# Zeroed sums and two borrowed weight places in the expert stage of a one-core trunk

## Chip, cores and metric

The kernel runs on one core of a Trainium2 chip. The metric is the device time of one launch in microseconds (us); lower is better. Before the change three timed runs gave 1368.88, 1369.80 and 1372.61 us, median 1369.8 us.

## What is computed

256 tokens of width 1024 pass a retention layer with a dense SwiGLU, and then an attention layer with a mixture of experts. The last part is what the change touches:

```python
logits = (xt @ w_router)                       # 256 tokens, 8 experts
top_val, top_idx = lax.top_k(logits, TOP_K)    # 2 of 8 for each token
gates = ...softmax of the two values...
for e in range(N_EXPERTS):                     # w_in[e]: 1024 x 7168, w_out[e]: 3584 x 1024, float32
    y = y + gates[:, e:e + 1] * swiglu(xt, w_in[e], w_out[e])
x = layer_norm(DEEPNORM_ALPHA * x + y)
```

The weights of the eight experts are 352 MB in float32, and every one of them is read once.

## The kernel before

**Experts, blocks and the flag.** For each expert the kernel gathers the rows (tokens) that chose it, at most 96 (CAP), as NB = 3 blocks of 32 rows. Blocks are the stationary operand of TensorE, weights are streamed past them. Block 2 (the third) is needed only where an expert has over 64 rows. That is known on the chip alone: VectorE writes a flag for each expert (`over`, `over_o`), TensorE loads it into a register (`third`), and `by_need` puts most of block 2's matmuls into a branch on it (L1195). The experts are taken in an order worked out on the chip (`which`), so their weights' addresses are registers.

**Units.** An expert's inner width of 3584 is cut into units of 2048 and 1536 columns (UNITS). A unit has a gate product `pg` and an up product `pu` (`gemm_e`, 8 steps of 128 rows of w_in each, tile `pe`, one PSUM bank a block), SiLU by ScalarE (L1266), a multiplication and a transpose by VectorE (L1288, L1290, tile `hT`), and the down product (`down`, 16 or 12 steps, tiles `po`, two banks for three blocks). The down product of a unit is issued after the up product of the next unit. Behind the second unit's down product `rows_of` copies the sums with ScalarE and VectorE (L1236 to L1243), and `scatter` adds them to `xa` one unit later. All matmuls of `gemm_e` and `down` are at L1176, in `mm_tiles`: 4 matmuls a step and block, which work on four column groups side by side. The profile counts each of them twice, since a float32 matmul is two instructions.

**`by_need`.** Steps are taken in groups (2 steps in the very first unit, else 4; 8 in the down product). In a group blocks 0 and 1 come first and then, in the branch, block 2. Step 0 is an exception: all three blocks run outside the branch, because its first matmul (start=True) is what sets block 2's sums to a value; its `done`, which gives the weight's place back, also comes ahead of the branch.

**Places and the stream of loads.** All weights pass through one `Stream`. A load is one DMA of 1 MB (or 0.75 MB, for the unit of 1536 columns), issued by SyncE (SP) at L217 in the order of use. `pump` issues a load as soon as a place is free; `Slots` counts the free places of a pool. Places come from `raws` (6), `raw_mid` (6), `raw_end` (3, free when the attention ends) and `base` (4, free when the attention's output product is done): 19 in the expert stage. A place is free again when the step that reads it is done. SP takes its list in order: a load that waits holds up all loads behind it. Loads use eight completion semaphores in turn, so a load also waits for the one eight before it.

**The attention's input.** `xT_h` and `xT_l` (1 MB each, pool `xtp`) hold the split, transposed input of the attention's products (L379 to L406). After the attention `xT_h`'s place is taken by `xa`, the residual of the last norm, written by ScalarE in `router_rest`, and `xT_l`'s place by `hT`.

**The end.** In the last expert TensorE adds `xa` into PSUM (L1304), runs the last down product, and scatters; VectorE and ScalarE then make the norm and store.

Of the kernel before, what the change touches and what calls it, by code (L numbers as in the profile page):

```python
# [23 lines left out]
P = 128  # L24
S = 256
D = 1024
# [71 lines left out]
class Slots:  # L98


    def __init__(self, pool, free, tag="raw"):
        self.pool, self.free, self.tag = pool, free, tag


class Stream:
# [78 lines left out]
def trunk_kernel(ctx, tc, x, ret_w_in, ret_w_out, sb_w_kv, sb_w_q, sb_w_out, ln_mix_g, ln_mix_b,  # L184
# [17 lines left out]
    def wtile(name="pw"):  # L202
        return psw.tile([P, 512], F32, tag="pw", name=nm(name))
# [665 lines left out]
    with att:  # L869
# [70 lines left out]
        for u in range(8):  # L940
            if u == 6:
                dst = [wtile("pv") for _ in range(2)]
                gemm_tok(dst, lambda t: keep_v(1, t, dst[t]))
            kq_half(u, 0)
            if u in (1, 2):
                att_a(u - 1)
            if u >= 2:
                att_c(u - 2)
            kq_half(u, 1)
            if u >= 2:  # L950
                att_e(u - 2)
                att_a(u)
        hl0 = st.take(4)
        acc0 = [wtile("sacc") for _ in range(2)]

# [21 lines left out]
        st.pump()  # L977


        xa = xtp.tile([P, 2, D], F32, tag="xT_h", name="xa")  # L980
        rt = mp.tile([P, P], F32, tag="gT0", name="rt")
        lg, rank, mask, ex = [rt[:, 64 + 16 * i:80 + 16 * i].rearrange("p (t e) -> p t e", t=2) for i in range(4)]
        mb = consts.tile([P, 2, NE], BF, name="mb")
# [141 lines left out]
        def router_rest():  # L1125

            nc.vector.tensor_scalar(mask, rank, 1.5, None, OP.is_lt)
            nc.vector.tensor_mul(ex, ex, mask)
            nc.vector.tensor_reduce(mx, ex, axis=AX.X, op=OP.add)
            nc.vector.reciprocal(mx, mx)  # L1130
            nc.vector.tensor_tensor(gates, ex, mx.rearrange("p (t o) -> p t o", o=1).to_broadcast((P, 2, NE)),
                                    OP.mult)
            nc.vector.tensor_reduce(nm_f, pc[:, :8], axis=AX.X, op=OP.max)
            nc.vector.tensor_copy(nmax, nm_f)
            turns()
            nc.vector.tensor_scalar(p2, p1, float(CAP), None, OP.subtract)
            for t in range(2):
                for n in range(2):
                    nc.vector.tensor_add(xs[t][:, half(n)], xs[t][:, half(n)], gb[1][n])
                nc.scalar.activation(xa[:, t, :], xs[t], AF.Copy, scale=ALPHA)  # L1140

        st.raws.append(base)
        st.pump()
# [3 lines left out]
        xg = gather_T(first)  # L1147
        nc.scalar.preload_act_table_set("silu_and_others")


    def slots(g, e, gates, last=False):

# [13 lines left out]
                nc.scalar.copy(gT[t], p[:, t * P:(t + 1) * P])  # L1166
        return gT, gs

    def mm_tiles(nb, o, lhs, cols, first, last, shared=False):

        for r in nb:
            for c, w in enumerate(cols):
                ov = o[r][c * 32:(c + 1) * 32]
                if len(w.shape) == 3:
                    ov = ov.rearrange("p (b j) -> p b j", j=w.shape[2])
                nc.tensor.matmul(ov, lhs[r], w, start=first and not (shared and r == 1), stop=last,  # L1176
                                 skip_group_check=True)

    def by_need(s, nk, group, third, mm):

        if third is None:
            for k in range(nk):
                mm(range(NB), k, s.take()[0])
                s.done()
            return
        for k0 in range(0, nk, group):
            ks = range(k0, min(k0 + group, nk))
            w = s.take(len(ks))  # L1190
            for k in ks:
                mm(range(NB - (k > 0)), k, w[k - k0])
            if k0 == 0:
                s.done()
            with tc.If(third > 0):  # L1195
                for k in ks:
                    if k > 0:
                        mm(range(NB - 1, NB), k, w[k - k0])
            for k in ks:
                if k > 0:  # L1200
                    s.done()

    def gemm_e(s, xg, n, third, group=4):


        o = [wtile("pe")[:, :n // 4] for _ in range(NB)]
        by_need(s, KD, group, third, lambda nb, k, w: mm_tiles(nb, o, [xg[:, r, k, :] for r in range(NB)], blocks(w, 64),
                                                        k == 0, k == KD - 1))
        return o

    def down(s, hT, nk, po, first, last, third):
        by_need(s, nk, 8, third, lambda nb, k, w: mm_tiles(nb, po, [hT[:, r, k, :] for r in range(NB)],
                                                        [w[:, c * 256:(c + 1) * 256] for c in range(4)],
                                                        first and k == 0, last and k == nk - 1, True))

    def alternate(o):

# [40 lines left out]
    def experts(s, pos, gates, g, xg, norm, hook=None, most=None, third0=None):  # L1258
        pend = done = po = None
        third = [third0] + [None] * (NE - 1)  # L1260
        for e in range(NE):
            for u, (c0, n) in enumerate(UNITS):
                hs = mp2.tile([P, NB, 512], F32, tag="hs", name=nm("hs"))[:, :, :n // 4]
                pg = gemm_e(s, xg, n, third[e], 2 if (e, u) == (0, 0) else 4)
                for r in range(NB):
                    nc.scalar.activation(pairs(hs[:, r, :]), alternate(pg[r]), AF.Silu)  # L1266
                if hook is not None:
                    hook()
                    hook = None
                if most is not None and (e, u) == (4, 0):  # L1270
                    most.append(nc.values_load(nmax[0:1, 0:1], min_val=0, max_val=S))
                if u == 1:
                    if done is not None:
                        scatter(*done)
                    sl = slots(g, e, gates, most is not None and e == NE - 1)
                    if e + 1 < NE:
                        if third0 is not None:
                            third[e + 1] = flag(over_o, e + 1)
                        g = one_hot(e + 1, pos)
                        nxt = gather(g)  # L1280
                pu = gemm_e(s, xg, n, third[e], 2 if (e, u) == (0, 0) else 4)
                if most is not None and (e, u) == (0, 0):
                    which[1:] = [nc.values_load(which_t[0:1, i:i + 1], engines=[SP], min_val=0, max_val=NE - 1,
                                                skip_runtime_bounds_check_because="a rank among NE")
                                 for i in range(1, NE)]
                hT = xtp.tile([P, NB, 16, 32], F32, tag="xT_l", name=nm("hT"))[:, :, :n // P]
                for r in range(NB):
                    nc.vector.tensor_mul(pairs(hs[:, r, :]), pairs(hs[:, r, :]), alternate(pu[r]))  # L1288
                for r in range(NB):
                    nc.vector.transpose(hT[:, r].rearrange("p k s -> p (k s)"), hs[:, r, :])  # L1290
                if pend is not None:
                    if pend[1] == 0:
                        po = new_po()
                    down(s, *pend[0], po, pend[1] == 0, pend[1] == 1, third[e - (u == 0)])
                    if pend[1] == 1:
                        done = (rows_of(po, sl[1]), sl[0])
                pend = ((hT, n // P), u)
            if e + 1 < NE:
                xg = nxt
        if most is not None:  # L1300
            sums = [[wtile("psc") for _ in range(2)] for _ in range(2)]
            for t in range(2):
                for n in range(2):
                    nc.tensor.matmul(sums[t][n], ident, xa[:, t, half(n)], start=True, stop=False)  # L1304
            tc.mark_branch_hint_location("more", 0, engines=[e for e in ENGINES if e != PE])
        down(s, *pend[0], po, False, True, third[NE - 1])
        if most is None:
            scatter(rows_of(po, sl[1]), sl[0], norm)
            for t in range(2):
                norm[t].fast_rstd(t == 1)  # L1310
            return None
        keep_warm(WARM[3], ident, ident)
        rows = rows_of(po, sl[1], True)
        for t in range(2):
            for n in range(2):
                nc.tensor.matmul(sums[t][n], sl[0][t][:CAP], rows[n][0], start=False, stop=True)
                nc.vector.bn_stats(norm[t].st[:, n, :], sums[t][n])
                nc.scalar.copy(xa[:, t, half(n)], sums[t][n])
            norm[t].fast_rstd(t == 1)
        return sums  # L1320

    norm = [Norm(t, [], xa[:, t, :]) for t in range(2)]
    for t in range(2):
        norm[t].st = small.tile([P, 2, 6], F32, tag="st", name=nm("st"))
    most = []
# [77 lines left out]
```

## Time and profile before

| What | Value |
|---|---|
| Median of the timed runs | 1369.8 us |
| Profiled execution, its own time | 1371.01 us |
| Its span (first to last instruction) | 1369.2 us |
| TensorE (PE) busy | 1325.5 us, 97% |
| VectorE (DVE), ScalarE (ACT) busy | 33%, 23% |
| DMA queue of SP | 442.01 MB, 82.8% of 16 engines |

The profile is one execution of the same program. PE busy means that a matmul was in the array or queued behind operands, so 97% is not a measure of how far the weights' loads leave TensorE waiting. The view by stretches gives, for each, busy time of every engine with the number of instructions, TensorE's granted clock (1.00 is 2.4 GHz, 0.50 is 1.2 GHz), the mean busy share of the 16 DMA engines and the bytes moved. A load's landing is the time of the last of its sixteen parts.

### The profile page before, as it was taken

The numbers are of one execution on the slowest core, as the hardware profiler recorded it, in microseconds if no ns is written. First come the engines' busy times: TensorE is split into PE (matmuls) and PEld (weight loads), VectorE is DVE, ScalarE is ACT, GpSimd is POOL, SyncE is SP. The second block draws the span as 40 slices with busy tenths as digits, with TensorE's granted clock in tenths as the row PEclk, the third lists the DMA queues.
The fourth block names the chain that finished last, engine by engine and source line by source line (L and its number), as shares of the span: only waits on it lengthen the run. The fifth ranks groups of instructions, "written<-read, shape, count | busy, mean of one in ns | idle before, by whom it ended". The sixth has DMA issues, their size and how long they took to land. (4 is left out here: it accounts for less than half of the span.)

```text
span 1369.2 us, 30767 instructions
## 1 busy us (share of the span) xinstructions
PE 1325.5 (97%) x13611; PEld 865.6 (63%) x13611; DVE 446.5 (33%) x652; ACT 314.8 (23%) x465; POOL 46.7 (3%) x73
## 2 busy tenths in 40 slices
PE   9999999999999999999989999999999999999986
PEld 7888889999989884354434454563644563554543
DVE  6746667555565554101201200201200200210213
ACT  6544435444437642000100100100100100100101
POOL 0212101000010000000000000000000000000000
PEclk9999999999999999999999999999999999999999
DMA  9865437555649357999999999999999999999993
GB/s 336 295 213 179 160 97 272 179 190 185 185 127 357 131 183 295 393 418 417 418 418 418 416 420 418 417 418 419 400 418 420 406 418 420 401 417 419 405 415 155
DMA packets 122918, 447.40 MB, mean 327 GB/s; under 512 B 9088, under 2 KB 56976, under 8 KB 92048
## 3 DMA queue, kind: packets, MB, share of 16 engines
q1 hardware_dynamic: 121808, 442.01, 82.8%
q0 software_dynamic: 960, 3.15, 0.7%
q8 instruction: 123, 2.02, 0.6%
q14 instruction: 27, 0.22, 0.0%
HBM read 444.08 MB, written 1.05 MB: 325 GB/s over the span
## 5 line engine op out<-in xcount | busy, mean ns | idle before, releaser
L1176 PE MATMUL pe<-raw,xg 128*32 128x384 f32 (+1 forms) x5248 | 506.3, 540 | 13.4 <-PEq L1195 7.4
L1176 PEld LDWEIGHTS pe<-raw,xg 128*32 128x32 f32 x5248 | 203.9, 110 | 305.4 <-issue 266.6
L1176 PE MATMUL po<-raw,hT 128*32 128x256 f32 x4544 | 254.4, 379 | 8.4 <-DMA raw<-in_moe_w_out_dram 5.4
L269 DVE TENSOR_TENSOR w<-raw,w 128x1024 fp32r<-128x1024 f32 x162 | 198.1, 1234 | 144.5 <-ACT w L268 142.2
L1176 PEld LDWEIGHTS po<-raw,hT 128*32 128x32 f32 x4544 | 170.0, 110 | 95.6 <-issue 10.7
L268 ACT CAST w<-raw 128x1024 fp32r<-128x1024 f32 x162 | 168.4, 1048 | 134.6 <-issue 32.1
L1288 DVE TENSOR_TENSOR hs<-hs,pe 128x512 f32<-128x512 f32 (+1 forms) x48 | 29.1, 620 | 362.9 <-PE pe L1176 361.2
L1266 ACT ACTIVATE hs<-pe 128x512 f32<-128x512 f32 (+1 forms) x48 | 25.3, 544 | 457.7 <-PE pe L1176 457.7
L404 PE MATMUL pf<-xT_h,w 128*128 128x256 f32 x448 | 126.9, 283 | 0.0
L406 PE MATMUL pf<-xT_l,w 128*128 128x256 f32 x448 | 126.2, 282 | 0.0
L405 PE MATMUL pf<-xT_h,w 128*128 128x256 f32 x448 | 126.1, 281 | 0.0
L1290 DVE STREAM_TRANSPOSE hT<-hs 128x512 f32<-128x512 f32 (+1 forms) x48 | 27.2, 617 | 237.6 <-PE po L1176 139.2
L404 PEld LDWEIGHTS pf<-xT_h,w 128*128 128x128 f32 x448 | 84.4, 188 | 0.3
L405 PEld LDWEIGHTS pf<-xT_h,w 128*128 128x128 f32 x448 | 84.4, 188 | 0.3
L406 PEld LDWEIGHTS pf<-xT_l,w 128*128 128x128 f32 x448 | 84.4, 188 | 0.0
L1236 ACT COPY y<-po 32x256 f32<-32x256 f32 x48 | 17.5, 364 | 283.3 <-PE po L1176 238.7
L379 PE MATMUL pv<-w,xT_l 128*128 128x512 f32 x96 | 38.4, 400 | 0.0
L381 PE MATMUL pv<-w,xT_h 128*128 128x512 f32 x96 | 38.0, 396 | 0.3 <-DVE w L269 0.3
L380 PE MATMUL pv<-w,xT_h 128*128 128x512 f32 x96 | 37.9, 395 | 0.0
L404 PE MATMUL pq<-xT_h,w 128*128 128x256 f32 x128 | 36.3, 283 | 0.0
L406 PE MATMUL pq<-xT_l,w 128*128 128x256 f32 x128 | 36.0, 281 | 0.0
L405 PE MATMUL pq<-xT_h,w 128*128 128x256 f32 x128 | 36.0, 281 | 0.0
(237 smaller groups left out, 1180.5 us busy)
## 6 DMA issues: line engine op xcount, KB each, us to landing
raw<-in_moe_w_in_dram SPq DMA_DIRECT2D x128, 1024.0 KB, 19.9
raw<-in_moe_w_out_dram SPq DMA_DIRECT2D x112, 1024.0 KB, 19.8
raw<-in_moe_w_in_dram SPq DMA_DIRECT2D x128, 768.0 KB, 15.8
raw<-in_ret_w_in_dram SPq DMA_DIRECT2D x22, 1024.0 KB, 9.3
raw<-in_ffn_w_in_dram SPq DMA_DIRECT2D x20, 1024.0 KB, 5.1
raw<-in_ffn_w_out_dram SPq DMA_DIRECT2D x11, 1024.0 KB, 5.0
raw<-in_ret_w_out_dram SPq DMA_DIRECT2D x8, 1024.0 KB, 5.0
raw<-in_sb_w_kv_dram SPq DMA_DIRECT2D x4, 1024.0 KB, 6.0
```

The lines of the kernel that those rows point to most:

```text
L268: nc.scalar.copy(hv, v)
L269: nc.vector.tensor_sub(lv, v, hv.bitcast(F32))
L379: nc.tensor.matmul(o, sl, mh, start=first, stop=False)
L380: nc.tensor.matmul(o, sh, mh, start=False, stop=False)
L381: nc.tensor.matmul(o, sh, ml, start=False, stop=last)
L404: nc.tensor.matmul(o, lo[:, k, :], xT_h[:, k, :], start=(k == 0), stop=False)
L405: nc.tensor.matmul(o, h[:, k, :], xT_h[:, k, :], start=False, stop=False)
L406: nc.tensor.matmul(o, h[:, k, :], xT_l[:, k, :], start=False, stop=(k == KD - 1))
L1176: nc.tensor.matmul(ov, lhs[r], w, start=first and not (shared and r == 1), stop=last, skip_group_check=True)
L1266: nc.scalar.activation(pairs(hs[:, r, :]), alternate(pg[r]), AF.Silu)
L1288: nc.vector.tensor_mul(pairs(hs[:, r, :]), pairs(hs[:, r, :]), alternate(pu[r]))
L1290: nc.vector.transpose(hT[:, r].rearrange("p k s -> p (k s)"), hs[:, r, :])
```

## The change

Three things are changed together.

1. *Zeroed sums.* Where there is a flag, VectorE sets block 2's sums to 0: 128x512 or 128x384 of a `pe` bank ahead of each `gemm_e`, and 128x256 of `po` ahead of the first unit's down product. Block 2's matmuls no longer start with start=True, and step 0's are in the branch with the others. All `done` of a group now come behind the branch.
2. *Two places more.* At the end of the attention two places of 1 MB, at `xT_l` and `xT_h`, are put among the `raws`. A `Once` place is given once: when its load has been used it does not come back.
3. *`xa` and `po` elsewhere in the order.* `xa` is made and written by ScalarE behind the up product of the first unit, not in `router_rest`; `new_po` comes ahead of the multiplications and transposes.

```diff
+class Once:
+    def __init__(self, pool, tag):
+        self.pool, self.tag, self._free = pool, tag, 1
...
+    @free.setter
+    def free(self, n):
+        self._free = min(self._free, n)
...
+        st.raws += [Once(xtp, tag) for tag in ("xT_l", "xT_h")]
+        st.pump()
         hl0 = st.take(4)
...
-                nc.scalar.activation(xa[:, t, :], xs[t], AF.Copy, scale=ALPHA)
...
+    def new_xa(norm):
+        nonlocal xa
+        xa = xtp.tile([P, 2, D], F32, tag="xT_h", name="xa")
+        for t in range(2):
+            norm[t].x = xa[:, t, :]
+            nc.scalar.activation(xa[:, t, :], xs[t], AF.Copy, scale=ALPHA)
...
             for k in ks:
-                mm(range(NB - (k > 0)), k, w[k - k0])
-            if k0 == 0:
-                s.done()
+                mm(range(NB - 1), k, w[k - k0])
             with tc.If(third > 0):
                 for k in ks:
-                    if k > 0:
-                        mm(range(NB - 1, NB), k, w[k - k0])
+                    mm(range(NB - 1, NB), k, w[k - k0])
             for k in ks:
-                if k > 0:
-                    s.done()
+                s.done()
...
         o = [wtile("pe")[:, :n // 4] for _ in range(NB)]
+        if third is not None:
+            nc.vector.memset(o[NB - 1], 0.0)
...
+                if pend is not None and pend[1] == 0:
+                    po = new_po()
+                    if third[e] is not None:
+                        nc.vector.memset(po[NB - 1], 0.0)
```

In the orders below a tile's number only tells copies apart, and line numbers of the changed kernel are its own (its L232 is L217 of before, L1200 is L1176, L1217 is L1195). The first place is SP's list at the end of the attention, with what each load waits for (DMAHW: an earlier load, DVE or PE: an engine). Before:

```order
L217 DMA raw_4372<-in_moe_w_in_dram 128x2048 [waits DMAHW5_49,DVE_49]
L217 DMA raw_4474<-in_moe_w_in_dram 128x2048 [waits DMAHW6_49,DVE_49]
L217 DMA raw_4568<-in_moe_w_in_dram 128x2048 [waits DMAHW7_49,DVE_49]
L217 DMA raw_4599<-in_moe_w_in_dram 128x2048 [waits DMAHW0_49,DVE_49]
L217 DMA raw_4617<-in_moe_w_in_dram 128x2048 [waits DMAHW1_49,PE_49]
L217 DMA raw_4619<-in_moe_w_in_dram 128x2048 [waits DMAHW2_49,PE_49]
```

And now:

```order
L232 DMA raw_4372<-in_moe_w_in_dram 128x2048 [waits DMAHW5_49,DVE_49]
L232 DMA raw_4474<-in_moe_w_in_dram 128x2048 [waits DMAHW6_49,DVE_49]
L232 DMA raw_4504<-in_moe_w_in_dram 128x2048 [waits DMAHW7_49,PE_49]
L232 DMA raw_4506<-in_moe_w_in_dram 128x2048 [waits DMAHW0_49]
L232 DMA raw_4572<-in_moe_w_in_dram 128x2048 [waits DMAHW1_49,DVE_49]
L232 DMA raw_4603<-in_moe_w_in_dram 128x2048 [waits DMAHW2_49,DVE_49]
```

Two loads (raw_4504, raw_4506) have come in behind the tenth load of the stage; they wait for TensorE's last reading of the attention's input. They are the eleventh and twelfth in the order of use; every later load stands two places further on in the list of places.

The second place is TensorE's list at the first gate product. Before:

```order
L1176 MATMUL pe_4857<-raw_3726,xg_4849 32x512 x4
L1176 MATMUL pe_4858<-raw_3726,xg_4849 32x512 x4
L1176 MATMUL pe_4859<-raw_3726,xg_4849 32x512 x4
L1176 MATMUL pe_4857<-raw_3808,xg_4849 32x512 x4
L1176 MATMUL pe_4858<-raw_3808,xg_4849 32x512 x4
L1195 COMPARE_AND_BRANCH
L1176 MATMUL pe_4859<-raw_3808,xg_4849 32x512 x4
```

And now:

```order
L1200 MATMUL pe_4860<-raw_3726,xg_4852 32x512 x4
L1200 MATMUL pe_4861<-raw_3726,xg_4852 32x512 x4
L1200 MATMUL pe_4860<-raw_3808,xg_4852 32x512 x4
L1200 MATMUL pe_4861<-raw_3808,xg_4852 32x512 x4
L1217 COMPARE_AND_BRANCH
L1200 MATMUL pe_4862<-raw_3726,xg_4852 32x512 x4
L1200 MATMUL pe_4862<-raw_3808,xg_4852 32x512 x4
```

Block 2's four matmuls of step 0 have moved behind the branch.

The third place is VectorE's list in the second unit of the sixth expert, between the transposes of the first unit's result and the gather of the next expert. Before:

```order
L1290 STREAM_TRANSPOSE hT_9698<-hs_9460 128x512 x3
L1236 COPY y_9863<-po_9248 32x256 x2
L1236 COPY y_9863<-po_9249 32x256
L1243 SCALAR_TENSOR_TENSOR y_9872<-y_9863,gs_9084,y_9871 96x512
L1236 COPY y_9864<-po_9248 32x256 x2
L1236 COPY y_9864<-po_9249 32x256
L1243 SCALAR_TENSOR_TENSOR y_9882<-y_9864,gs_9084,y_9881 96x512
L1195 UNCONDITIONAL_BRANCH x2
L1254 TENSOR_TENSOR xa<-xa,psc_10006 128x512
```

And now:

```order
L1317 STREAM_TRANSPOSE hT_9725<-hs_9485 128x512 x3
L1258 COPY y_9890<-po_9265 32x256 x2
L1258 COPY y_9890<-po_9266 32x256
L1265 SCALAR_TENSOR_TENSOR y_9899<-y_9890,gs_9107,y_9898 96x512
L1258 COPY y_9891<-po_9265 32x256 x2
L1258 COPY y_9891<-po_9266 32x256
L1265 SCALAR_TENSOR_TENSOR y_9909<-y_9891,gs_9107,y_9908 96x512
L1228 MEMSET pe_9915 128x384
L1217 UNCONDITIONAL_BRANCH x2
L1276 TENSOR_TENSOR xa<-xa,psc_10034 128x512
```

The zeroing of the second unit's gate sums (pe_9915) stands behind the transposes and all of `rows_of`.

## Rows read from the trace of the kernel before

**Rows 1.** The page: span; busy us (share) xcount; GB/s in 40 slices.

```profile
span 1369.2 us, 30767 instructions
...
PE 1325.5 (97%) x13611; PEld 865.6 (63%) x13611; DVE 446.5 (33%) x652; ACT 314.8 (23%) x465; POOL 46.7 (3%) x73
...
GB/s 336 295 213 179 160 97 272 179 190 185 185 127 357 131 183 295 393 418 417 418 418 418 416 420 418 417 418 419 400 418 420 406 418 420 401 417 419 405 415 155
```

**Rows 2.** Stretches: busy us (x), PE to POOL; then PEclk, DMA share, GB/s.

```profile
494.00:500.00 6.00, 6.00 (x35) 4.63 (x34) 2.26 (x3) 3.11 (x5) 0.00 (x0) 1.00 0.00 0
...
520.00:524.00 4.00, 3.89 (x46) 2.16 (x45) 2.15 (x11) 0.30 (x1) 0.00 (x0) 0.57 1.03 422
...
526.00:530.00 4.00, 3.86 (x48) 1.27 (x44) 2.93 (x16) 0.97 (x1) 0.00 (x0) 1.00 0.00 0
...
546.00:562.00 16.00, 15.17 (x144) 4.98 (x140) 3.05 (x5) 0.45 (x1) 0.00 (x0) 1.00 0.98 357
...
700.00:1340.00 640.00, 622.91 (x8068) 319.71 (x8060) 88.91 (x169) 44.22 (x102) 0.00 (x0) 1.00 1.01 415
...
1344.00:1348.00 4.00, 3.95 (x76) 2.09 (x67) 0.00 (x0) 0.00 (x0) 0.00 (x0) 1.00 0.50 199
```

**Rows 3.** Waits of SP's queue, 494 to 563: us in total, times, longest.

```profile
SPq L217 <- PEq L1195: 20.8, 8, 3.5
SPq L217 <- PE pe L1176: 15.8, 2, 13.8
```

**Rows 4.** Waits of SP's queue, 590 to 1345.

```profile
SPq L217 <- DMA raw<-in_moe_w_in_dram: 376.7, 222, 3.4
```

**Rows 5.** End of the run: weight loads of TensorE, 1349 to 1351.

```profile
1349.86 1.23 PEld L1176 LDWEIGHTS po<-raw,hT 128*32 128x32 f32 x27 [0.28 <-DMA raw<-in_moe_w_out_dram]
```

**Rows 6.** The page: matmuls of the experts, count, busy us, mean ns, idle before.

```profile
L1176 PE MATMUL pe<-raw,xg 128*32 128x384 f32 (+1 forms) x5248 | 506.3, 540 | 13.4 <-PEq L1195 7.4
...
L1176 PE MATMUL po<-raw,hT 128*32 128x256 f32 x4544 | 254.4, 379 | 8.4 <-DMA raw<-in_moe_w_out_dram 5.4
```

**Rows 7.** TensorE's last reading of the attention's input: start us, us.

```profile
485.40 0.28 PE L406 MATMUL pf<-xT_l,w 128*128 128x256 f32 x1
```

**Rows 8.** SP's issues, four single ones in order of time: start us, us.

```profile
488.32 0.33 SPq L217 DMA_DIRECT2D raw<-in_moe_w_in_dram  x1
...
552.04 0.33 SPq L217 DMA_DIRECT2D raw<-in_moe_w_in_dram  x1
...
552.46 0.38 SPq L217 DMA_DIRECT2D raw<-in_moe_w_in_dram  x1
...
555.85 0.33 SPq L217 DMA_DIRECT2D raw<-in_moe_w_in_dram  x1
```

**Rows 9.** Loads issued at 488.32, 529.97, 548.23, 552.04: KB, us to landing.

```profile
raw<-in_moe_w_in_dram SPq DMA_DIRECT2D x1, 1024.0 KB, 4.9
...
raw<-in_moe_w_in_dram SPq DMA_DIRECT2D x1, 768.0 KB, 4.2
...
raw<-in_moe_w_in_dram SPq DMA_DIRECT2D x1, 768.0 KB, 8.6
...
raw<-in_moe_w_in_dram SPq DMA_DIRECT2D x1, 768.0 KB, 8.7
```

**Rows 10.** VectorE in the fourth expert, second unit: transposes and last of `rows_of`.

```profile
867.04 1.90 DVE L1290 STREAM_TRANSPOSE hT<-hs 128x512 f32<-128x512 f32 x3 [14.78 <-PE po L1176]
...
874.86 0.75 DVE L1243 SCALAR_TENSOR_TENSOR y<-y,gs,y 96x512 fp32r<-96x512 f32 x1 [0.85 <-ACT y L1242]
```

**Rows 11.** TensorE at the same place: the gate product of that unit.

```profile
866.77 15.69 PE L1176 MATMUL pe<-raw,xg 128*32 128x384 f32 x192
```

**Rows 12.** The only kind of zeroing in the trace before, on VectorE.

```profile
529.75 0.06 DVE L1105 MEMSET rt<- 128x1 f32 x1
```

**Rows 13.** Waits of TensorE in the last expert, 1203 to 1337.

```profile
PE po L1176 <- DMA raw<-in_moe_w_out_dram: 3.2, 4, 1.9
```

**Rows 14.** TensorE's last down product, its first eight steps.

```profile
1340.40 7.55 PE L1176 MATMUL po<-raw,hT 128*32 128x256 f32 x136
```

More of the change, by code (lines that the diff above doesn't have):

```diff
@@ L102, in __init__, with free @@
         self.pool, self.free, self.tag = pool, free, tag
+class Once:
+    def __init__(self, pool, tag):
+        self.pool, self.tag, self._free = pool, tag, 1
+    @property
+    def free(self):
+        return self._free
+    @free.setter
+    def free(self, n):
+        self._free = min(self._free, n)
 class Stream:
@@ L977, in trunk_kernel @@
         st.pump()
-        xa = xtp.tile([P, 2, D], F32, tag="xT_h", name="xa")
+        xa = None
         rt = mp.tile([P, P], F32, tag="gT0", name="rt")
@@ L1167, in slots, with mm_tiles @@
         return gT, gs
-    def mm_tiles(nb, o, lhs, cols, first, last, shared=False):
+    def mm_tiles(nb, o, lhs, cols, first, last, shared=False, zeroed=False):
         for r in nb:
@@ L1175, in mm_tiles @@
                     ov = ov.rearrange("p (b j) -> p b j", j=w.shape[2])
-                nc.tensor.matmul(ov, lhs[r], w, start=first and not (shared and r == 1), stop=last,
+                nc.tensor.matmul(ov, lhs[r], w, start=first and not (shared and r == 1) and not (zeroed and r == NB - 1),
+                                 stop=last,
                                  skip_group_check=True)
@@ L1191, in by_need @@
             for k in ks:
-                mm(range(NB - (k > 0)), k, w[k - k0])
-            if k0 == 0:
-                s.done()
+                mm(range(NB - 1), k, w[k - k0])
             with tc.If(third > 0):
                 for k in ks:
-                    if k > 0:
-                        mm(range(NB - 1, NB), k, w[k - k0])
+                    mm(range(NB - 1, NB), k, w[k - k0])
             for k in ks:
-                if k > 0:
-                    s.done()
+                s.done()
     def gemm_e(s, xg, n, third, group=4):
         o = [wtile("pe")[:, :n // 4] for _ in range(NB)]
+        if third is not None:
+            nc.vector.memset(o[NB - 1], 0.0)
         by_need(s, KD, group, third, lambda nb, k, w: mm_tiles(nb, o, [xg[:, r, k, :] for r in range(NB)], blocks(w, 64),
-                                                        k == 0, k == KD - 1))
+                                                        k == 0, k == KD - 1, False, third is not None))
         return o
@@ L1213, in down @@
                                                         [w[:, c * 256:(c + 1) * 256] for c in range(4)],
-                                                        first and k == 0, last and k == nk - 1, True))
+                                                        first and k == 0, last and k == nk - 1, True, third is not None))
     def alternate(o):
@@ L1282, in experts @@
                 if most is not None and (e, u) == (0, 0):
+                    new_xa(norm)
                     which[1:] = [nc.values_load(which_t[0:1, i:i + 1], engines=[SP], min_val=0, max_val=NE - 1,
@@ L1291, in experts @@
                 if pend is not None:
-                    if pend[1] == 0:
-                        po = new_po()
                     down(s, *pend[0], po, pend[1] == 0, pend[1] == 1, third[e - (u == 0)])
@@ L1320, in experts @@
         return sums
-    norm = [Norm(t, [], xa[:, t, :]) for t in range(2)]
+    norm = [Norm(t, [], xs[t]) for t in range(2)]
     for t in range(2):
```

## Prediction, written before the result was known

> **What bounds the kernel now.** I read the page's slices first. From about 550 us to the last slice the weights arrive at 400 to 420 GB/s; ahead of that there are slices at 131 to 295 [rows 1]. TensorE is busy 97% over the whole span, which by itself would name it the bound. The stretches decide: from 700 to 1340 us the sixteen DMA engines are busy 1.01 of the time at 415 GB/s, TensorE 623 of 640 us [rows 2]. So both are nearly full, and the next question is which of them waits last. The queue of SP, from 590 us to the end, waits 222 times for an earlier load (its semaphore of eight), 376.7 us, with hardly a wait for a place [rows 4]; and the last weights are awaited by TensorE, not the other way round: 0.28 us on the DMA at 1349.86 [rows 5]. In the last expert TensorE waits four times, 3.2 us, for data [rows 13]. So the stream of loads sets the end, and a change is worth what it moves of that stream.
>
> The stream is not full everywhere. At 494 to 500 and 526 to 530 us the DMA share is 0.00 [rows 2]. There SP's queue waits for places, not for the DMA: 15.8 us for a matmul, the longest 13.8, and 20.8 us in eight waits for the branch of `by_need` [rows 3]. All 19 places are filled before the first product has given one back.
>
> **Two places more.** TensorE reads the attention's input last at 485.40 plus 0.28 us [rows 7], and SP issues its load before the new ones at 488.32 [rows 8]. The two new loads, 1 MB each, stand next in the list and need only that reading, so they start at about 489, with 4.9 us to landing as the one before them [rows 9]; the forerunner lands at 493.2, and 2 x 1.05 MB / 0.415 = 5.1 us later, at about 498, they are in: in time in which nothing moved. They shift all later loads by two positions in the list of places: what is now issued at 552.04 and 552.46 into the places of the eleventh and twelfth load finds no place there, since `Once` gives none back; the next issue is the one at 555.85 [rows 8].
>
> What is it worth? These two later issues carry 0.786 MB each (768 KB). At 415 GB/s [rows 2] that is 2 x 0.786 / 0.415 = 3.8 us of transfer that has left the full stretch. The whole 3.8 is had only if the queue stays full across the place where they stood. At 546 to 562 us the share is 0.98 [rows 2], so there is just about enough queued. The load issued at 548.23 takes 8.6 us to land, at 556.8 [rows 9]; a load on an empty queue takes 4.2 [rows 9], so the one issued at 555.85, if it is 0.9 us earlier (below), lands at 559.2 at the earliest, while with the queue full it would land 1.9 us (0.786 / 0.415) behind its forerunner's 556.8 less 0.9, at 557.8. The gap of 1.4 us is an upper bound, as a load's parts overlap with the next one's on sixteen engines that don't run dry together; I take half of it, 0.6 to 0.7.
>
> **Zeroed sums: the matmuls.** Four matmuls on one block are eight rows of the profile. In a gate or up product that is 8 x 506.3 / 5248 = 0.77 us, in a down product 8 x 254.4 / 4544 = 0.45 us [rows 6]. An expert whose block 2 is empty saves step 0 in four gate and up products, and in its two down products, 4 x 0.77 + 2 x 0.45 = 4.0 us. The counts of rows tell how many such experts there are: 5248 / 8 = 656 groups are 68 for each small expert and 96 for each large one, so 4 of each (which ones, a product's rows tell: 192 in the fourth [rows 11], 136 in the last one's first eight steps [rows 14], which is two blocks and a third block once). In sum TensorE saves 4 x 4.0 = 16 us, 192 rows. Beside a full DMA it is worth nothing by itself: what hides it is the stream's 415 GB/s, and TensorE only waits longer for data.
>
> It counts in one place, the first unit, where the stream still waits for TensorE's releases [rows 3]. There the first product is 0.87 us shorter (step 0's block 2, a little above the mean, since the clock was granted 0.57 shortly before, at 520 to 524 [rows 2]), and behind the up product it is 2 x 0.87 = 1.75. The loads that fill the gap behind 526 to 530 are started by the first release, so I take 0.87; 1.75 is the upper end. Step 0's place is now given back with its group's instead of alone; the first release is later by one step of two blocks, but the group's second goes with it, and the two are loads of one queue. I cost that at nothing; if it is uncovered it takes away the 0.87.
>
> **Zeroing and its wait.** There are 40 zeroings on VectorE. The only kind in the trace is 128x1 at 0.06 us [rows 12]; the nearest of the size is the 96x512 multiply-add at 0.75 us [rows 10]. I take 0.5 us, nearer to the second since the size is. VectorE is 33% busy [rows 1], so 40 x 0.5 = 20 us cost nothing as work. Where they stand matters. In a large expert's second unit the zeroing for the gate product stands behind the three transposes and all of `rows_of`, and the branch's first matmul waits for it. In the fourth expert the transposes start at 867.04 and the last instruction of `rows_of` ends at 874.86 + 0.75 = 875.6 [rows 10]; the zeroing ends at 876.1. TensorE starts that product at 866.77 and passes a block's four steps each 15.69 / 6 = 2.6 us [rows 11], so it is at block 2 after two of them, at 872.0. It waits 4.1 us (3.6 if zeroing is free, 4.4 at 0.75), in each of the four large experts. Behind it stand the rest of the gate product and all later matmuls, and the releases of eight places. SP has places to spare then [rows 4], so the stream does not wait; TensorE is 4.1 us later per large expert, 16 us in all, against 16 saved in the small ones. Order counts: the small experts are 1, 2, 5 and 8. Of the lateness of the sixth and seventh, 8.2 us, the last can make good its 3.2 us of waits [rows 13] and the 4.0 it saves, 7.2 in all. Left are 0 to 1 us at the end.
>
> The Trainium skill ("VectorE: DVE Perf Modes", section "Zero memsets can be issued as uint32 (trn2)") says that a zeroing takes one cycle per element; from that I estimate some 0.4 to 0.55 us for 384 or 512 elements. The sum would be the same by it; no run yet shows it.
>
> `xa`'s two copies of 128x1024 go behind the first up product on ScalarE, which is 23% busy [rows 1]; nobody reads them before the first scatter. By 0.75 us for 96x512 [rows 10] I estimate 3 us for both; uncovered they would delay the next unit's SiLU by that, and a gate product of over 10 us [rows 11] hides them. `new_po` earlier than the transposes costs nothing, the banks being long read by then.
>
> **Sum.** 3.8 - 0.65 + 0.87 = 4.0 us gained; TensorE's remainder at the end takes 0 to 1 of it, and I take 0. On the profiled execution, 1371.0 us (a span of 1369.2 and 1.8 around it), that makes 1367.0. The median of the runs, 1369.8, is 1.2 lower; 4.0 off it gives **1365.8 us**. Bounds: 1.75 us gained if the two places win nothing (they come on top of the nineteen, so I see no loss in them) and only the shorter products count, 3.8 + 1.75 = 5.5 if the queue never runs dry. A measurement of this kernel tells a difference of about 0.3%, 4.1 us, from none, so the forecast lies on that border.
>
> **Rivals.**
> - *The queue stays full across 552 to 556 us.* For it: the share of 0.98 there. Against: 8.6 us to landing means that only two or three loads were queued. Gain 5.5, time 1364.3. Chance 0.20.
> - *The lead is lost.* The stream waits for places at TensorE's pace until some 560 us, and with two places fewer behind them the two loads' lead becomes an idle queue. For it: the waits for the branch [rows 3]. Against: the share of 0.98. Gain 1.75, time 1368.0. Chance 0.22.
> - *TensorE becomes the bound behind VectorE.* Place: block 2 of the second unit's gate product in the third, fourth, sixth and seventh experts. It decides from 1 us more lateness per expert on, since only 7.2 us can be made good in the last. At 3 us more, say by a zeroing that waits for the bank's last reader as well, the sixth and seventh bring 2 x 7.1 - 7.2 = 7 us against the 4.0 gained: 3 us slower, 1372.8. For it: TensorE at 623 of 640 us has little air. Against: the transposes and `rows_of` are the same work as before. Chance 0.07.
> - *The clock falls.* TensorE's granted clock was 0.57 at 520 to 524 us, after the router's waits, but 1.00 over all of 700 to 1340, with waits of up to 1.9 us [rows 2, 13]. The new waits are 4.1. If they halve the clock in the last expert, the last down product's first eight steps take 7.55 us more [rows 14] and the other four half of that: 11 us, less the 4.0: 1377. Chance 0.04. [...]
> - *Matmul time is paid in full*, the bound being TensorE after all, and the new waits lie in its idle time: 16 us, 1354. The wait at the end [rows 5] is against it. Chance 0.03.
>
> **How the numbers follow.** The forecast (gain 2.9 to 5) has 0.44. Faster by over 0.3%: just under half of the forecast's (0.20), the full queue (0.20), matmul time (0.03): 0.43. Slower by over 0.3%: the clock's 0.04 and half of TensorE's 0.07, whose price grows by 2 us with each further microsecond: 0.07. The rest, 0.50, is within. The range of 8 in 10 goes from 1362.8 (the full queue, and the runs' own spread of 1.5) to 1369.3 (the lead lost, with 1.3 of the same); the forecast's own is 1364.5 to 1367.
>
> **What would show it.** Two loads at about 489 us that land before 500; none at 552.04 and 552.46; the idle stretch at 526 to 530 remains; the last weights land about 4 us earlier. 192 fewer matmul rows, 40 zeroings. Four waits of TensorE for VectorE's zeroing, 2 to 4 us each, in the large experts' second gate product. I am wrong if the last wait of TensorE is not on the DMA, if the idle stretches at 494 or 530 widen by as much as the two loads fill, or if the share between 546 and 562 falls below 0.9.

## The result, and the profile after

The changed kernel is slower: 1381.55 us median of 7 runs (1374.9 to 1386.42) beside 1370.38 for the kernel before (7 runs), ratio 1.0063 with a 95% interval of 1.0044 to 1.0083 (here and below the ratio is taken over all runs and is not the quotient of the two medians). Forecast were 1365.8 and a range up to 1369.3. The profiled execution is the fastest of the seven, 1374.9 us with a span of 1373.1.

The page of the changed kernel: span; busy us (share) xcount by engine; GB/s in 40 slices. It answers to [rows 1].

```profile
span 1373.1 us, 30400 instructions
...
PE 1314.3 (96%) x13419; PEld 850.1 (62%) x13419; DVE 462.4 (34%) x692; ACT 314.5 (23%) x465; POOL 46.7 (3%) x73
...
GB/s 339 295 211 182 153 109 259 184 184 184 184 143 347 127 262 299 377 417 416 418 419 417 418 418 417 418 405 418 416 418 419 410 418 419 387 379 420 414 419 90
```

The counts are as forecast: 192 rows of matmuls fewer, 40 instructions more on VectorE. TensorE has 11 us less work and the profiled execution ends 4 us later. New is a dip to 387 and 379 GB/s in the two slices from 1167 to 1236 us: the stream, which had run at 400 to 420 GB/s to the last slice, is held up there.

The stretches of the changed kernel, in the columns of [rows 2] (us; busy us and count of PE, PEld, DVE, ACT, POOL; granted clock, DMA share, GB/s):

```profile
494.00:500.00 6.00, 6.00 (x34) 4.92 (x34) 2.63 (x3) 3.24 (x5) 0.00 (x0) 1.00 0.49 208
520.00:524.00 4.00, 3.99 (x85) 2.72 (x89) 3.16 (x13) 0.22 (x1) 0.00 (x0) 1.00 0.71 288
526.00:530.00 4.00, 3.82 (x40) 1.21 (x36) 3.38 (x20) 0.00 (x0) 0.00 (x0) 1.00 0.03 6
546.00:562.00 16.00, 15.17 (x156) 5.42 (x152) 4.42 (x9) 2.00 (x2) 0.00 (x0) 1.00 0.86 324
700.00:1340.00 640.00, 613.26 (x7936) 309.00 (x7928) 98.44 (x194) 44.14 (x102) 0.00 (x0) 0.99 1.01 413
872.00:876.00 4.00, 2.64 (x20) 0.87 (x24) 1.13 (x2) 0.07 (x1) 0.00 (x0) 0.59 1.02 419
1080.00:1084.00 4.00, 4.00 (x36) 1.48 (x32) 0.00 (x0) 0.00 (x0) 0.00 (x0) 0.62 1.01 409
1200.00:1204.00 4.00, 3.68 (x28) 1.24 (x32) 0.27 (x1) 0.00 (x0) 0.00 (x0) 0.57 0.66 235
```

Three things stand in them. The two loads fill part of the stretch from 494 to 500. The share of 546 to 562 has fallen from 0.98 to 0.86, so part of what they won is idle again there. And in three places of the expert stage, where the clock was 1.00 throughout, a stretch of 4 us now has 0.57 to 0.62 of it. The cause stands ahead of each; here TensorE in the fourth expert (start, us, engine, line, op, tiles, count, idle before and what ended it):

```profile
864.02 5.37 PE L1200 MATMUL pe<-raw,xg 128*32 128x384 f32 x64
873.36 11.89 PE L1200 MATMUL pe<-raw,xg 128*32 128x384 f32 x128 [3.98 <-DVE pe L1228]
```

In the third, sixth and seventh expert the same place reads:

```profile
754.44 10.53 PE L1200 MATMUL pe<-raw,xg 128*32 128x384 f32 x128 [3.16 <-DVE pe L1228]
...
1079.70 12.22 PE L1200 MATMUL pe<-raw,xg 128*32 128x384 f32 x128 [3.54 <-DVE pe L1228]
...
1200.32 12.22 PE L1200 MATMUL pe<-raw,xg 128*32 128x384 f32 x128 [3.98 <-DVE pe L1228]
```

And VectorE in the fourth expert, which answers to [rows 10]:

```profile
864.28 1.90 DVE L1317 STREAM_TRANSPOSE hT<-hs 128x512 f32<-128x512 f32 x3 [14.79 <-PE po L1200]
...
872.10 0.75 DVE L1265 SCALAR_TENSOR_TENSOR y<-y,gs,y 96x512 fp32r<-96x512 f32 x1 [0.85 <-ACT y L1264]
872.93 0.38 DVE L1228 MEMSET pe<- 128x384 f32 x1
```

The zeroing takes 0.38 us, and TensorE has waited 3.98 for it. Then 128 rows (matmul instructions) take 11.89 us. In [rows 11] the same 192 rows ran without a break in 15.69, that is 10.5 for 128. TensorE's waits from 560 us to the end, by line and what it waited for (us in total, times, longest):

```profile
PE pe L1200 <- DVE pe L1228: 14.7, 4, 4.0
```

At the end TensorE no longer waits for the last weights; compare [rows 5]. Its weight loads in the last down product, and those of them that read the last load, from 1353.64 us on:

```profile
1344.84 6.63 PEld L1200 LDWEIGHTS po<-raw,hT 128*32 128x32 f32 x128 [0.76 <-issue]
1352.11 3.21 PEld L1200 LDWEIGHTS po<-raw,hT 128*32 128x32 f32 x64 [0.63 <-issue]
```

```profile
1353.65 1.67 PEld L1200 LDWEIGHTS po<-raw,hT 128*32 128x32 f32 x32
```

SP's queue from 590 to 1345 waits for TensorE too, which [rows 4] had hardly shown:

```profile
SPq L232 <- DMA raw<-in_moe_w_in_dram: 299.9, 184, 3.4
...
SPq L232 <- PE pe L1200: 54.4, 22, 11.2
SPq L232 <- PE po L1200: 34.0, 21, 8.2
```

The bound has changed sides. In the trace before, the last load landed at 1349.82 and was read at 1349.86. Now it lands at 1345.23, 4.6 us earlier, and is read at 1353.65. TensorE is 8.4 us behind its data. That is nearly all of the 3.9 us by which the span has grown: 8.4 of lateness less the 4.6 by which the data come earlier.

Of those 4.6 us, 1.9 are chance, not the change. The first expert product starts at 525.21, against 527.12 before:

```profile
525.21 3.64 PE L1200 MATMUL pe<-raw,xg 128*32 128x512 f32 x32
```

That comes from the router, where the clock in this execution stayed at 1.00 from 520 to 524 (0.57 in [rows 2]); it is seen below that executions of one kernel differ in this by up to 4.7 us. From the first product to the last landing it is 822.7 us before and 820.0 now: the change is worth 2.7 us to the stream in this pair of profiles (1.3 in the second profile below).

### The profile page after: what moved, and what is told of

It is laid out like the page before. It is cut to its first block, busy times and chain, and to the rows that moved or that the text cites. A ratio compares the mean times of both kernels' runs of the same rounds, so it can differ in the third digit from the quotient of the medians.

```text
span 1373.1 us, 30400 instructions
## 1 busy us (share of the span) xinstructions
PE 1314.3 (96%) x13419; PEld 850.1 (62%) x13419; DVE 462.4 (34%) x692; ACT 314.5 (23%) x465; POOL 46.7 (3%) x73
## 5 line engine op out<-in xcount | busy, mean ns | idle before, releaser
L1200 PE MATMUL pe<-raw,xg 128*32 128x512 f32 (+1 forms) x5120 | 499.3, 544 | 26.8 <-DVE pe L1228 14.7
L1200 PEld LDWEIGHTS pe<-raw,xg 128*32 128x32 f32 x5120 | 189.2, 111 | 326.6 <-issue 281.2
L1200 PE MATMUL po<-raw,hT 128*32 128x256 f32 x4480 | 250.9, 379 | 9.5 <-DMA raw<-in_moe_w_out_dram 4.3
L1200 PEld LDWEIGHTS po<-raw,hT 128*32 128x32 f32 x4480 | 169.4, 110 | 94.0 <-issue 14.9
L1276 DVE TENSOR_TENSOR xa<-xa,psc 128x512 f32<-128x512 f32 x28 | 17.4, 682 | 58.5 <-PE psc L1275 58.5
L419 PE MATMUL pq<-xT_h,w 128*128 128x256 f32 x128 | 36.3, 283 | 0.0
```

The source lines that it names most:

```text
L419: nc.tensor.matmul(o, lo[:, k, :], xT_h[:, k, :], start=(k == 0), stop=False)
```

## The experiments

All kernels were timed against the kernel before; ratios are with their 95% intervals. They fall into three groups, by the median of the kernel before that was timed beside them: 1370.26 us for the places alone, the zeroed sums alone, the early zeroing and the filled wait; 1370.15 for the zeroing between the halves, in the first expert, and early without the places; 1373.43 for the early zeroing's second timing and for the zeroing between the halves and in the first expert without the places. Between groups, ratios and not times are to be compared. The theory W: TensorE waits for VectorE's zeroing in the large experts' second gate product, loses clock behind the wait, and so becomes the bound. Its rivals are named in the expectations.

**The places alone** (with `xa` and `po` moved as in the change). Block 2 as in the kernel before; the zeroing of `po` goes too:

```diff
-                mm(range(NB - 1), k, w[k - k0])
+                mm(range(NB - (k > 0)), k, w[k - k0])
+            if k0 == 0:
+                s.done()
...
-        if third is not None:
-            nc.vector.memset(o[NB - 1], 0.0)
```

> The two places more (and xa, po moved), with block 2 as in the kernel before: step 0 outside the branch, no zeroing, step 0's place back ahead of the branch. Theory W (TensorE waits for VectorE's zeroing in the large experts' second gate product, 14.7 us in four waits, and loses clock behind three of them; the places themselves gain): no such waits, granted clock 1.00 over 700 to 1340, all loads about 4 us earlier than before (5.0 in the changed kernel, less the 0.9 of a shorter first product), end on the DMA: 1366, range 1364.5 to 1367.5. Rival P (the two places that do not come back, or the longer list, hold the stream back later): SP waits for TensorE in the expert stage as in the changed kernel and the time is 1373 to 1382.

Measured: 1369.37 us, ratio 0.9994 (0.9974 to 1.0013). No loss, so rival P falls; but no gain either, against W's 1366. None of the waits that W names is there (the clock is 1.00 over 700 to 1340, and falls once before, at 694), and the last load is awaited by TensorE (landed 1349.07, read 1349.11). The stretches (columns as above):

```profile
530.00:546.00 16.00, 15.07 (x137) 5.18 (x133) 6.27 (x25) 1.68 (x3) 0.00 (x0) 1.00 0.84 297
546.00:562.00 16.00, 15.17 (x144) 4.96 (x140) 2.37 (x4) 2.00 (x2) 0.00 (x0) 1.00 0.80 299
```

The lead of the two loads has become idle time of the DMA, 0.80 in place of 0.98. The issues of SP at that place (start us, us):

```profile
548.91 0.33 SPq L232 DMA_DIRECT2D raw<-in_moe_w_in_dram  x1
...
556.53 0.33 SPq L232 DMA_DIRECT2D raw<-in_moe_w_in_dram  x1
```

Between them are 7.6 us without an issue: the load at 556.53 waits for the same release as the one at 555.85 before [rows 8].

**The zeroed sums alone**, without the line that adds the two places.

> The zeroed sums alone, without the two places. Theory W: the four waits on the zeroing (14 to 16 us in all) and the fall of the clock stay; the loads are only 1 to 1.75 us earlier than before, so TensorE meets its last data some 4 us later than in the changed kernel and carries the same two last waits behind it: 1382 to 1387, slower than the changed kernel. Rival P: 1368.5 to 1370, as the places are not there.

Measured: 1377.7 us, ratio 1.0059 (1.0035 to 1.0083). Rival P expected 1368.5 to 1370 and falls for good. W's sign is right, its size of 1382 to 1387 too high: the kernel is not slower than with the places. Its trace has four waits of 14.4 us in all for the zeroing, and 12.04, 12.22 and 12.22 us for the 128 rows behind three of them.

**Zeroing early.** The banks of the second unit's gate product are taken ahead of the transposes, and `gemm_e` is given them:

```diff
...
+                if u == 0 and pend is not None:
+                    ahead = new_pe(UNITS[1][1], third[e])
                 hT = xtp.tile([P, NB, 16, 32], F32, tag="xT_l", name=nm("hT"))[:, :, :n // P]
```

> The changed kernel with one move: the banks of the second unit's gate product are taken, and block 2's zeroed, ahead of the multiplications and transposes of the first unit instead of behind rows_of. Theory W: TensorE's waits on the zeroing are gone (under 1 us in all), granted clock 1.00 from 700 to 1340, last data awaited by TensorE, the stream 5.0 us earlier than before: 1365.4, range 1364 to 1367. Rival R (places are given back later, behind the branch, and that starves the stream; the waits on the zeroing are idle time): still 1375 to 1382, with SP waiting over 100 us for TensorE after 590. Rival P: 1373 to 1382 too.

Measured: 1370.04 us, ratio 0.9989 (0.997 to 1.0008). With the zeroing (and the taking of its banks) moved, the loss is gone, so it came with the wait. R and P fall. W's 1365.4 is missed by 4.6.

**The same, a second time**, beside other kernels:

> The kernel that zeroes early, with both places, once more beside the two others, since its first 12 runs (median 1370.0, from 1365.7 to 1373.3) stood on another chip job than the kernels near 1367. Theory: it is not different from them, 1366 to 1370, and its runs fall into earlier and later ones by the clock in the router, 516 to 535 us. Rival (where the zeroing stands ahead of the multiplications it delays them, and that costs 2 to 3 us): 1369.5 to 1371 again, above both others.

Measured: 1368.2 us, ratio 0.9968 (0.9947 to 0.9989); this is inside W's 1366 to 1370 and 0.8 and 0.9 us above the two others of its group, so the rival's 2 to 3 us for delayed multiplications is not seen; a smaller cost is not excluded. Its profile is the best partner of the changed kernel's, since its first product starts at 525.21 too, and its last load lands at 1345.29, against 1345.23. The last weights in it, and the span:

```profile
1345.33 1.45 PEld L1200 LDWEIGHTS po<-raw,hT 128*32 128x32 f32 x32 [1.00 <-DMA raw<-in_moe_w_out_dram]
```

```profile
core 0: 1364.6 us, clock 0.997
```

With its first product and its last data at the same times it ends at 1364.6 in place of 1373.1: TensorE's lateness is 8.5 us of time.

**The wait filled with work.** 14 idle matmuls stand in the branch, ahead of block 2:

```diff
             with tc.If(third > 0):
+                if fill and k0 == 0:
+                    keep_warm(fill, ident, ident)
...
```

> The changed kernel with 14 idle matmuls of 128x128 (0.26 us each, 3.7 us) at the head of the branch of block 2 in the second unit's gate product, in large experts alone: TensorE is as late as with the wait, but it is not idle in it. Theory W with the clock as a part: the granted clock stays 1.00 from 700 to 1340, the profile ends some 3.5 us earlier than the changed kernel's (two cold stretches of 1.76 us behind its last two waits): 1368 to 1372 in the timed runs, and the runs lie closer together than the 11.5 us of the changed kernel. Theory W without the clock (the wait alone costs, the clock's fall is an accompaniment): 1378 to 1383, the runs as far apart as before.

Measured: 1369.73 us, ratio 0.9991 (0.9973 to 1.001), runs from 1366.87 to 1374.88. TensorE in the fourth expert:

```profile
866.63 5.37 PE L1200 MATMUL pe<-raw,xg 128*32 128x384 f32 x64
871.93 3.39 PE L449 MATMUL warm<-ident 128*128 128x128 f32 x28
875.98 10.53 PE L1200 MATMUL pe<-raw,xg 128*32 128x384 f32 x128 [0.65 <-DVE pe L1230]
```

The matmuls of block 2 begin as late behind the first part as in the changed kernel, by 3.98 us, but the 128 rows take 10.53. TensorE ends 2.9 us behind its data (landed 1345.88, read 1348.75) in place of 8.4. So the wait's length costs about 3 us and the clock behind it the greater part, 5.5 by this difference; the cold time on record is 4.7 (below), so the split between two executions is a rough one. The rival without the clock (1378 to 1383) falls.

**The changed kernel once more**, for a second profile.

> The changed kernel once more, for a second profile, since its timed runs spread over 11.5 us with a mean granted clock of 0.993 to 0.982. If the clock is the cause of that spread, a slower execution shows the same four waits of about 4 us on the zeroing and longer or more stretches at 0.50 behind them: per 0.001 of mean clock about 1.0 to 1.4 us. If the waits themselves vary, they are longer than 4 us in the slower execution at the same cold time. Time 1375 to 1386.

Measured: 1383.3 us. TensorE behind the three waits of 3.98, 3.54 and 3.98 us:

```profile
878.37 13.38 PE L1200 MATMUL pe<-raw,xg 128*32 128x384 f32 x128 [3.98 <-DVE pe L1228]
...
1086.60 13.37 PE L1200 MATMUL pe<-raw,xg 128*32 128x384 f32 x128 [3.54 <-DVE pe L1228]
...
1208.36 12.22 PE L1200 MATMUL pe<-raw,xg 128*32 128x384 f32 x128 [3.98 <-DVE pe L1228]
```

These three waits are the same to the hundredth (the one in the third expert is 1.57 here, against 3.16), the cold time differs: over 10.53 each, 2.85 + 2.84 + 1.69 = 7.4 us, against 1.36 + 1.69 + 1.69 = 4.7 in the first profile (11.89, 12.22, 12.22). The other part of the spread is the router's. Its stretches in this execution:

```profile
516.00:520.00 4.00, 4.00 (x34) 3.97 (x34) 2.62 (x10) 2.55 (x4) 1.04 (x3) 0.87 1.01 406
520.00:524.00 4.00, 4.00 (x34) 1.61 (x38) 1.81 (x10) 0.14 (x1) 0.00 (x0) 0.50 0.76 313
524.00:528.00 4.00, 4.00 (x57) 2.84 (x61) 1.94 (x7) 1.50 (x2) 0.00 (x0) 0.50 0.00 0
528.00:532.00 4.00, 4.00 (x33) 1.25 (x28) 2.29 (x8) 0.00 (x0) 0.00 (x0) 0.50 0.00 0
```

The first product starts at 529.91 then, 4.7 us later than in the first profile, and every release and load behind it is later. This part is not of the change alone: the kernels with the early or middle zeroing show it as well (first product at 525.21, 529.57 and 530.13). The runs of the kernel before spread over 1367 to 1377 us, with mean clocks from 0.998 to 0.991; that they do so by the router too is likely, but only one of them has a profile.

**Zeroing between the halves of `rows_of`:**

```diff
             out_.append((yh, yl))
+            if between is not None and n == 0:
+                between()
...
+                        def between():
+                            nonlocal ahead
+                            ahead = new_pe(UNITS[1][1], third[e])
```

> The changed kernel with the zeroing of the second unit's gate sums between the two halves of rows_of instead of behind both: it ends about 0.5 us after TensorE gets to block 2, so four waits of 0.3 to 1 us are left. Theory W with the clock (a wait of 4 us costs its length and a cold stretch; a short one its length alone, and the last expert's slack takes that): granted clock 1.00 from 700 to 1340, 1369 to 1371.5. Rival L (any wait on VectorE at that place costs a cold stretch): 1374 to 1379.

Measured: 1366.6 us, ratio 0.997 (0.9954 to 0.9985): faster than the kernel before and the changed one, and below W's 1369 to 1371.5. TensorE in the fourth expert:

```profile
871.79 10.53 PE L1200 MATMUL pe<-raw,xg 128*32 128x384 f32 x128 [0.63 <-DVE pe L1226]
```

A wait of 0.63 us costs no clock; rival L falls. Without the two places (mid_zero):

> The kernel that zeroes between the halves of rows_of (1366.6), without the two places. Theory (the lead of the two places is lost, what gains is the first expert's shorter products): no difference to it, 1365.5 to 1368.5. Rival (the places are worth what their two loads carry, 3.8 us): 1369.5 to 1371.5.

Measured: 1367.41 us, ratio 0.9957 (0.994 to 0.9974).

**Zeroing in the first expert alone**; step 0 outside the branch in the other seven:

```diff
-                mm(range(NB - 1), k, w[k - k0])
+                mm(range(NB - (k > 0 or zeroed)), k, w[k - k0])
...
+                pg = gemm_e(s, xg, n, third[e], 2 if (e, u) == (0, 0) else 4, third[e] is not None and e == 0)
```

> Zeroing and late release in the first expert alone; the other experts run step 0 of all three blocks outside the branch, as before. The two places stay. No wait on a zeroing is then possible in the large experts. Theory W, its second half (with the waits gone the stream of loads sets the end, and saved matmuls count only in the first expert): 1369 to 1371, as the kernel that zeroes early (1370.0). Rival M (TensorE is so near the bound that the 12 us saved in the other small experts count too): 1373 to 1378.

Measured: 1366.99 us, ratio 0.9976 (0.9961 to 0.9991). Rival M (1373 to 1378) falls: the time of the other experts' saved matmuls is worth nothing that shows. The expected 1369 to 1371 is missed as well, by 2 us on the fast side. Without the places (first_zero):

> Zeroing in the first expert alone (1367.0 with the two places), without the places: nothing is left of the change but the first expert's saved step-0 matmuls, xa and po elsewhere. Theory: the same time, 1365.5 to 1368.5. Rival (the places gain): 1369.5 to 1371.

Measured: 1367.26 us, ratio 0.9963 (0.9948 to 0.9978).

**Zeroing early, without the places:**

> The kernel that zeroes early (1370.0), without the two places. Theory: the lead of the two loads is lost, since from the twelfth release on a load waits for the same release as before; only the shorter first products move the stream: 1369 to 1371.5, no difference to the kernel with the places. Rival (the places keep what the two later loads carry, 3.8 us): 1373 to 1375.

Measured: 1367.91 us, ratio 0.998 (0.9965 to 0.9996). The rival's 1373 to 1375 falls; the 1369 to 1371.5 expected is missed by 1.1. In all three pairs (0.997 and 0.9957, 0.9976 and 0.9963, 0.9989 or 0.9968 and 0.998) the intervals overlap, and the places show no gain; one of an us or so is not excluded. The stretch that tells, in the kernel with the zeroed sums alone (columns as above):

```profile
546.00:562.00 16.00, 15.17 (x152) 5.45 (x152) 4.42 (x9) 0.00 (x0) 0.00 (x0) 1.00 1.02 414
```

In the four kernels with zeroed sums and without the places the share there is 1.00 to 1.02, in all those with the places 0.80 to 0.90, whenever the first product started: the places put idle time there that was elsewhere before.

## Why the prediction was wrong, step by step

**The step that failed** is "TensorE's remainder at the end takes 0 to 1 of it, and I take 0": it is 8.4 us. The wait itself was read rightly: four waits at the place named, 14.7 us against 4 x 4.1, and the zeroing at 0.38 us (0.485 for 512 columns) against 0.5. (The Trainium skill, "VectorE: DVE Perf Modes", section "Zero memsets can be issued as uint32 (trn2)", states one cycle per element; the estimate of 0.4 to 0.55 for 384 or 512 elements that the prediction made from it lies a little above these times.) What was left out of that step is what a wait does to the matmuls behind it. Each of three waits of 3.5 to 4.0 us makes the next 128 rows 1.4 to 2.9 us longer. The fourth, 3.16 us in the third expert, costs none in the profile; there the matmuls behind it take 10.53. With 4.7 to 7.4 us of this on top, the last expert's slack no longer does, and TensorE ends 8.4 us behind its data in the first profile and 10.7 in the second. Two of the prediction's own signs of being wrong are there: the last wait of TensorE is not on the DMA, and the share of 546 to 562 is below 0.9.

**The remainder without the clock** was too small as well: 2.9 us in the kernel with the filled wait, not 0 to 1. The working let the fifth expert make good the whole lateness of the third and fourth. In that kernel's trace the sixth expert's second gate product finds its data 3.7 us earlier than before (landed 1067.12 against 1070.83), but TensorE comes to it only 0.75 us earlier (1071.34 against 1072.09). So it is 4.2 us behind its data there, against 1.3 before: the fifth expert has not made good all of the lateness.

**Two rivals were each half of it.** "TensorE becomes the bound behind VectorE" (0.07) named the right place, and "the clock falls" (0.04) the right mechanism, but at the end of the last expert, and by halving a whole product. They were priced apart. Together they need no more waiting than was worked out, since the cold time comes on top of it. The clock had its small chance since waits of up to 1.9 us had left it at 1.00. The Trainium skill ("TensorE: Matmul & The Clock Gate", section "HAM oscillation — how this bites in real kernels") tells of a clock that falls behind waits for the DMA; the runs agree with it at 3.5 to 4.0 us, though what is waited for here is VectorE. The 0.57 at 520 to 524 us, which the prediction puts "after the router's waits", is no case of this: the trace before shows TensorE busy 3.89 of 4.00 us there and 4.00 of 4.00 from 516 to 520.

**The two places.** "3.8 - 0.65" is wrong, and the rival "the lead is lost" (0.22) right. The loads did start at 488.38 and 488.89 and had landed by 497.75, as forecast, but the DMA share of 546 to 562 fell to 0.86, and to 0.80 with the places alone. A share of 0.98 was read as a queue that is just full; it was one that just keeps pace with TensorE's releases. Here two places that give nothing back only moved the same waits.

**The shorter first products** were probably mis-sized the other way: 0.87 taken, 1.75 as the upper end. From the first product to the last landing the kernels with zeroed sums need 818.7 to 821.4 us against 822.7, 1.3 to 4.0 less (the places alone, without shorter products, 821.4 too); the one with zeroing in the first expert alone gains 0.0024 of the time, 3.3 us, with an interval of 1.2 to 5.3, and without the places 0.0037. The reason is probably the one above: the stream is at TensorE's pace for all products of the first unit and into the second's, not only until the first release. No run tries that by itself.

**Right were** the counts, the saved 16 us as worth nothing beside a full DMA (zeroing in the first expert alone is as good), the idle stretch of 526 to 530 that remains, and `xa` and `po`, for which no run shows a cost (the places alone have them too and lose nothing; none has them by themselves).

Not settled: why the medians differ by 11 us where the two profiled spans differ by 4. How long the cold stretches get in the slowest runs of the changed kernel is in no profile; the mean granted clock falls from 0.993 to 0.982 over its seven runs, and the time rises with it, though not run by run, from 1374.9 to 1386.42.

## What to carry to other kernels

An instruction put at the end of another engine's queue is priced by all that stands ahead of it, and a wait of TensorE by its length and by the clock behind it; here the zeroing put four VectorE instructions earlier, between the halves of `rows_of`, turned 0.6% of loss into a gain of 0.3%. Loads that start earlier are worth something only if the queue is full from there on: look for what the load behind them waits for. In this kernel saved matmuls counted at the start, where the stream is fed at TensorE's pace, and not where the DMA is full: one expert's worth of the edit had all of the gain.

## What the runs showed of the hardware

The granted clock fell behind all nine waits of 3.54 and 3.98 us in the three profiles that have them (two of the changed kernel, one of the zeroed sums alone), and the same 128 rows then took 11.89 to 13.38 us in place of 10.53; the same wait did not always cost the same. It did not fall behind waits of 0.63 to 3.16 us at the same place. But the length alone doesn't tell: with the places alone it fell behind one wait of 2.11 us for a transpose, at 694, and in the changed kernel a wait of 2.04 for data, at 682, left it at 1.00. The stretches around the former (columns as above):

```profile
692.00:696.00 4.00, 1.89 (x16) 0.45 (x12) 1.50 (x3) 0.00 (x0) 0.00 (x0) 0.80 1.01 420
696.00:700.00 4.00, 4.00 (x32) 1.12 (x28) 0.00 (x0) 0.00 (x0) 0.00 (x0) 0.77 1.01 412
```

In the router the clock fell without idle time that the profile shows: TensorE is busy 4.00 of 4.00 us in each stretch from 516 to 532 in the second profile, with a clock of 0.50 to 0.87, while it runs matmuls of 8 columns, the gather and some others; in the first profile it stays at 1.00 there. With 14 matmuls of 128 columns in the wait it stayed at 1.00 from 700 to 1340 us.
